# Scattered rows added on VectorE behind the gate products of the last expert pairs, the results of the last two groups summed in PSUM, tokens scaled during the output projection

## The chip, the core and the metric

The kernel runs on one core of one Trainium2 chip. The metric is the device time of one execution in microseconds, here called us; lower is better. Five engines work side by side and meet at semaphores: TensorE (PE, with its weight loads as PEld), VectorE (DVE), ScalarE (ACT), GpSimd (POOL) and SyncE (SP). SP issues nearly all loads of weights; POOL issues the gathers and scatters of rows whose place is known only at run time.

## The reference

Two layers work on 256 latent and 256 context tokens, each 1024 wide. A layer first mixes tokens (attention and a long convolution, left out here) and then runs a mixture of 32 experts, two for each token:

```python
x = x + g1 * _merge(attn, hyena, gates, w_br_a, w_br_b, w_out)      # output projection
h2 = _rms(x, norm_ffn) * (1.0 + sc2) + sh2                          # scaled tokens
x = x + g2 * _hier_moe(h2, w_group, b_group, w_router, b_router, moe_w1, moe_w3, moe_w2)
...
# for every expert e, with cw = the routing weight of the token for e
hid = silu(h2 @ w1[e]) * (h2 @ w3[e]) * cw
y = y + hid @ w2[e]
```

All is float32. Layer 0 does this for the latent and the context tokens, layer 1 for the latent tokens alone.

## The kernel before

**Tiles.** Tokens stand in tiles of 128 rows: four in layer 0 (tiles 0 and 1 latent, 2 and 3 context), two in layer 1. The output projection runs in two halves of 512 columns; for each half and tile, PE leaves a product in PSUM, DVE multiplies it by the gate `g1` and adds it to `x`, PE transposes `x`, multiplies it by the router's weights, and ACT squares it for the norm.

**Routing.** `moe` then forms `rs` (one over the root mean square) and the logits `lg`, runs a chain of small operations on DVE (all called `rtr` in the trace), and sends the scaled tokens `h2` to DRAM: `x*rs*sc2` by DVE, except for the last tile, which ACT and POOL do, and for every tile the addition of `sh2` by POOL. The chain ends in `gi`, the row numbers with which POOL gathers `xg`, the rows of one quad of experts, back from DRAM.

**Experts.** `first_round` walks over 8 quads q of 4 experts, that is 16 pairs of experts, counted here as p = 0 to 15 (quad q has the pairs 2q and 2q+1). For each pair, `w13` multiplies the gathered rows by two weights (PE, L1414, into `pW`), ACT takes `sl`, DVE forms the gate product `hd` (L1369, in `hidden`), PE transposes it into `pX` (L1372), ACT copies it to `hdT`, and `w2` multiplies by the third weight (PE, L1429). For q < 6 ACT copies the result `Y` to SBUF and POOL scatters its rows to `ybuf` in DRAM. After that, `collect` gathers them for each token tile (two DMAs of 512 KB: `yr` for even tiles of layer 0, `yt` for the rest), POOL adds the two (L220 on POOL), and DVE multiplies by `g2` (`bc`) and adds to `x`. For q = 6 and 7 nothing is scattered: `combine` multiplies `Y` by a matrix `PT` of zeros and ones on PE (L1462, into the PSUM banks G and Q), each quad for itself, and `residual` multiplies that by `g2` and adds it to `x` (`xg` and `x` of 512 columns on DVE).

**Order.** The code is given to a scheduler that fixes each engine's order beforehand; every engine then takes its instructions strictly in that order. A weight of 1 MB (96 in a layer) is loaded by `fetch` into the next slot of a ring as soon as the slot's last reader has been issued. The ring has 14 slots in layer 0 and 16 in layer 1. `yt` and the tokens `h2` share a pool of two buffers (`T4`).

## Time and profile before

| | |
|---|---|
| Time, median of 3 runs | 1466.85 us (1466.72 to 1468.5) |
| Profiled execution | 1467.82 us, of which span 1466.0 us |
| PE, DVE, ACT, POOL busy | 88%, 46%, 31%, 17% of the span |
| Mean granted PE clock | 0.954 of full speed |
| Experts of layer 0 | about 611 to 907 us of the span |
| Experts of layer 1 | about 1211 to 1457 us |

The busy shares are means over stages with different limits. In the middle of both expert stages the DMA engines are saturated and PE is hardly ever idle; at their ends this is not so, and there one has to look at which wait ends last. Times below are positions in the span, in us.

### The profile page before, as it was taken

The page shows a single profiled execution, that of the slowest core. Times are in us where ns is not written, and L with a number is a line of the kernel's source. Part 1 is how long each engine was busy: PE and PEld are TensorE (multiplying, and loading weights), DVE is VectorE, ACT ScalarE, POOL GpSimd, SP SyncE. Part 2 cuts the span into 40 slices and gives each one's busy share as a digit, 9 for nine tenths or more (in the row PEclk, how much of TensorE's full clock was granted, in tenths as well). Part 3 has the DMA queues.
Part 4 walks back from the last instruction along what each step waited for, and adds up shares of the span by engine and source line. Part 5 has one row for each costly group of instructions (what it writes and reads, how often), then busy time and mean ns, then how long its engine had stood idle before and what let it go on. Part 6 is the DMA issues. An engine that isn't in the chain of part 4 may idle for free. (4 is left out here: it accounts for less than half of the span.)

```text
span 1466.0 us, 18236 instructions
## 1 busy us (share of the span) xinstructions
PE 1294.2 (88%) x7071; PEld 831.8 (57%) x7071; DVE 672.0 (46%) x1365; ACT 450.8 (31%) x882; POOL 255.2 (17%) x193
## 2 busy tenths in 40 slices
PE   5999999999999999499988487899899949998886
PEld 2555778876577987244322123899779933433232
DVE  4654366666677655601000235774774771000014
ACT  3433222336622232122111002543575412221110
POOL 2021042360000003311101301122600031111010
PEclk8999999999999999599999788999999979999999
DMA  9645534554278663699999943343426757999992
GB/s 377 270 167 193 209 113 161 186 224 173 86 253 306 230 258 141 218 403 420 419 420 423 418 166 122 128 144 145 173 73 232 252 181 292 421 418 419 421 417 106
DMA packets 65691, 373.04 MB, mean 254 GB/s; under 512 B 11994, under 2 KB 13338, under 8 KB 26048
## 3 DMA queue, kind: packets, MB, share of 16 engines
q1 hardware_dynamic: 54368, 347.67, 60.9%
q0 software_dynamic: 10368, 21.02, 3.9%
q10 hardware_dynamic: 864, 3.15, 0.5%
q8 instruction: 57, 0.93, 0.2%
q14 instruction: 34, 0.28, 0.1%
HBM read 362.06 MB, written 27.53 MB: 266 GB/s over the span
## 5 line engine op out<-in xcount | busy, mean ns | idle before, releaser
L1414 PE MATMUL pW<-we,xT 128*64 128x512 f32 x1024 | 265.7, 609 | 13.1 <-DMA we<-in_wexp_dram 12.9
L1414 PEld LDWEIGHTS pW<-we,xT 128*64 128x64 f32 x1024 | 80.1, 139 | 158.0 <-issue 135.6
L1369 DVE SCALAR_TENSOR_TENSOR hd<-sl,cws,pW 128x256 f32<-128x256 f32 x32 | 15.3, 479 | 326.0 <-ACT sl L223 326.0
L239 PE MATMUL pA<-hT,wsp 128*128 128x512 f32 (+1 forms) x448 | 156.7, 350 | 3.9 <-ACT hf L223 3.9
L241 PE MATMUL pA<-hT,wsp 128*128 128x512 f32 (+1 forms) x448 | 154.8, 345 | 1.1 <-DVE wsp L220 1.1
L240 PE MATMUL pA<-hT,wsp 128*128 128x512 f32 (+1 forms) x448 | 154.5, 345 | 0.0
L220 DVE TENSOR_TENSOR wsp<-win,wsp 128x1024 fp32r<-128x1024 f32 x80 | 100.9, 1269 | 107.8 <-ACT wsp L223 107.6
L1429 PE MATMUL pW<-we,hdT 128*64 128x512 f32 x512 | 141.3, 616 | 4.9 <-ACT hdT L223 4.7
L223 ACT ACTIVATE wsp<-win 128x1024 fp32r<-128x1024 f32 x80 | 84.0, 1057 | 139.8 <-PE pA L241 136.2
L240 PE MATMUL pA<-wsp,hT 128*128 128x256 f32 x352 | 100.4, 285 | 2.5 <-DVE wsp L220 2.5
L239 PE MATMUL pA<-wsp,hT 128*128 128x256 f32 x352 | 100.8, 286 | 0.7 <-ACT vv L223 0.7
L241 PE MATMUL pA<-wsp,hT 128*128 128x256 f32 x352 | 100.4, 285 | 0.0
L239 PEld LDWEIGHTS pA<-hT,wsp 128*128 128x128 f32 x448 | 86.3, 193 | 21.7 <-issue 8.0
L240 PEld LDWEIGHTS pA<-hT,wsp 128*128 128x128 f32 x448 | 86.3, 193 | 13.8 <-issue 6.1
L241 PEld LDWEIGHTS pA<-hT,wsp 128*128 128x128 f32 x448 | 86.2, 192 | 11.3 <-issue 1.8
L1429 PEld LDWEIGHTS pW<-we,hdT 128*64 128x64 f32 x512 | 47.7, 141 | 74.1 <-issue 60.0
L223 ACT ACTIVATE sl<-pW 128x256 f32<-128x256 f32 x32 | 12.3, 384 | 238.0 <-PE pW L1414 238.0
L223 ACT ACTIVATE Y<-pW 128x512 f32<-128x512 f32 (+1 forms) x64 | 38.2, 598 | 141.0 <-PE pW L1429 125.0
L239 PEld LDWEIGHTS pA<-wsp,hT 128*128 128x128 f32 x352 | 68.1, 194 | 5.3 <-issue 2.5
L240 PEld LDWEIGHTS pA<-wsp,hT 128*128 128x128 f32 x352 | 68.1, 193 | 3.4 <-DVE wsp L220 3.1
L248 POOL TENSOR_TENSOR rs<-rsq,mh 128x1 f32<-128x1 f32 x14 | 11.6, 830 | 332.8 <-DVE rsq L247 331.8
L241 PEld LDWEIGHTS pA<-wsp,hT 128*128 128x128 f32 x352 | 68.2, 194 | 0.2
(301 smaller groups left out, 2377.6 us busy)
## 6 DMA issues: line engine op xcount, KB each, us to landing
we<-in_wexp_dram SPq DMA_DIRECT2D x190, 1024.0 KB
win<-in_win_dram SPq DMA_DIRECT2D x40, 1024.0 KB
ada<-in_ada_dram SPq DMA_DIRECT2D x32, 1024.0 KB
ada<-in_adaj_dram SPq DMA_DIRECT2D x16, 1024.0 KB
wbr<-in_wbr_dram SPq DMA_DIRECT2D x8, 1024.0 KB
wout<-in_wout_dram SPq DMA_DIRECT2D x8, 1024.0 KB
ybuf<-zero SPq DMA_DIRECT2D x12, 512.0 KB
bc<-modd SPq DMA_DIRECT2D x12, 512.0 KB
```

The lines of the kernel that those rows point to most:

```text
L220: (eng or self.nc.vector).tensor_tensor(out=out, in0=a, in1=b, op=op)
L223: self.nc.scalar.activation(out, in_, func, **kw)
L239: self.nc.tensor.matmul(out, lh, rh, start=start, stop=False)
L240: self.nc.tensor.matmul(out, lh, rl, start=False, stop=False)
L241: self.nc.tensor.matmul(out, ll, rh, start=False, stop=stop)
L248: nc.gpsimd.tensor_tensor(out=out, in0=t, in1=self.mh[:, : shape[1]], op=ALU.pow)
L1369: nc.vector.scalar_tensor_tensor(out=hd, in0=sl, scalar=cws, in1=pa[:, 256:512], op0=ALU.mult, op1=ALU.mult)
L1414: nc.tensor.matmul(pa[64 * e : 64 * e + 64, :], xT[:, kc, cs], wt[(2 * p + e, kc // 4)][:, kc % 4, :], start=kc == 0, stop=kc == KC - 1)
L1429: nc.tensor.matmul(py[64 * e : 64 * e + 64, :], hdT[:, fc, 64 * e : 64 * e + 64], wt[(2 * p + e, 2)][:, fc, hs], start=fc == 0, stop=fc == 1)
```

## The change

The change has six parts. (1) The tokens `h2` are formed in the loop of the output projection, on DVE alone; the loads of `sc2` and `sh2` come there too. (2) The two first `xg` buffers are zeroed by ACT (a copy with scale 0) instead of a POOL memset. (3) `collect` handles one tile at a time and returns the additions as a function; the two gathered halves are added on DVE. The gathers of the first half of the tiles are issued as before, after the second weight of pair 12; their additions are written behind `hidden` of pair 14. The gathers of the other tiles are written there too, and their additions behind `hidden` of pair 15. `g2` is loaded later. (4) The ring of layer 0 has slot 0 as a fifteenth for its first four rounds. (5) For tiles 0 and 1 the products of quads 6 and 7 are summed in one PSUM bank each, which is held from quad 6 to the end; for tiles 2 and 3 all eight products are done at the end. There is one `residual` for each tile and half in place of two. (6) Slots of some split weights change.

```diff
@@ output projection
+        h2 = [sc2b[:, i // 2, :] if i % 2 else self.T4([P, D], name="h2") for i in range(nt)]
...
                 self.tt(x_, x_, xg, ALU.add)
+                self.tt(h2[i][:, hs], x_, sc2b[:, i // 2, hs], ALU.mult)
...
+                if half:
+                    self.tt(ssq[i][:, 0:1], ssq[i][:, 0:1], ssq[i][:, 1:2], ALU.add)
+                    self.rsq(rss[i], ssq[i][:, 0:1], D, [P, 1])
+                    V.scalar_tensor_tensor(out=h2[i], in0=h2[i], scalar=rss[i], in1=sh2b[:, i // 2, :],
+                                           op0=ALU.mult, op1=ALU.add)
+                    nc.scalar.dma_start(self.rows[l][i * P : i * P + P, :], h2[i])
+                    V.scalar_tensor_tensor(out=lg[:, i, :], in0=lg[:, i, :], scalar=rss[i], in1=bb[:, i // 2, :],
+                                           op0=ALU.mult, op1=ALU.add)
@@ moe
-            if i < nt - 1:
-                V.scalar_tensor_tensor(out=h2, in0=x_, scalar=rss[i], in1=sc_, op0=ALU.mult, op1=ALU.mult)
-            else:
-                self.act(h2, x_, scale=rss[i])
-                self.tt(h2, h2, sc_, ALU.mult, nc.gpsimd)
-            self.tt(h2, h2, sh2b[:, i // 2, :], ALU.add, nc.gpsimd)
-            nc.scalar.dma_start(hd2[i * P : i * P + P, :], h2)
@@ pull
-                nc.gpsimd.memset(xg, 0.0)
+                self.act(xg, self.ones[:, 0:1].unsqueeze(2).to_broadcast([P, 2, D]), scale=0.0)
@@ collect
-                self.tt(ya, ya, yt[1], ALU.add, nc.gpsimd)
-                self.tt(ya, ya, g2[:, i // 2, :], ALU.mult)
-                self.tt(x_, x_, ya, ALU.add)
+            def add():
+                x_ = xm[i // 2][:, i % 2, :]
+                self.tt(yt[0], yt[0], yt[1], ALU.add)
+                self.tt(yt[0], yt[0], g2[:, i // 2, :], ALU.mult)
+                self.tt(x_, x_, yt[0], ALU.add)
+            return add
@@ first_round
             ring = [10, 11, 12, 13, 19, 20, 4, 5, 6, 7, 8, 9, 16, 18]
+            seq = (ring + [0]) * 4 + ring * 3
...
+        def add(q, i, half):
+            hs = slice(half * 512, half * 512 + 512)
+            for j in range(2):
+                for x in range(2):
+                    nc.tensor.matmul(held[i, half], quads[q]["PT"][j][:, i, :], quads[q]["Y"][j][:, x, hs],
+                                     start=q == 6 and j + x == 0, stop=q == 7 and j + x == 2)
...
             hdT = self.hidden(w13(2 * q, z["xT"], fill), z["cw"][:, 0:1])
+            if q == 7:
+                for u in adds:
+                    u()
+                adds = [collect(i) for i in range(nt // 2, nt)]
...
             if q == 6:
-                collect()
+                adds = [collect(i) for i in range(nt // 2)]
...
             hdT = self.hidden(w13(2 * q + 1, z["xT"], fill), z["cw"][:, 1:2])
+            if q == 7:
+                for u in adds:
+                    u()
...
-        for u in fill + last[6:] + combine(7):
+        for u in fill:
             u()
+        for i, half in units:
+            add(7, i, half)
+            residual(i, half, held[i, half], 7)
+        for i in range(2, nt):
+            for half in range(2):
+                held[i, half] = self.ps("G" if i == 2 else "Q")
+                for q in (6, 7):
+                    add(q, i, half)
+                residual(i, half, held[i, half], 7)
```

The diff does not tell where the scheduler puts these instructions. On DVE, in layer 0, from the gate product of pair 11 to that of pair 13 or just before it, the order was this (`x_4404` holds tiles 0 and 1, `x_4407` tiles 2 and 3):

```order
L1369 SCALAR_TENSOR_TENSOR hd_6037<-sl_6035,cws_5462,pW_5991 128x256
L220 TENSOR_TENSOR yr_6131<-yr_6131,bc_5008 128x1024
L220 TENSOR_TENSOR x_4404<-x_4404,yr_6131 128x1024
L1369 SCALAR_TENSOR_TENSOR hd_6123<-sl_6121,cws_5629,pW_6077 128x256
L220 TENSOR_TENSOR yt_6137<-yt_6137,bc_5008 128x1024
L220 TENSOR_TENSOR x_4404<-x_4404,yt_6137 128x1024
L220 TENSOR_TENSOR Y_6130<-pW_6159,Y_6130 128x512
L220 TENSOR_TENSOR Y_6130<-pW_6168,Y_6130 128x512
L220 TENSOR_TENSOR yr_6131<-yr_6131,bc_5008 128x1024
L220 TENSOR_TENSOR x_4407<-x_4407,yr_6131 128x1024
L220 TENSOR_TENSOR yt_6149<-yt_6149,bc_5008 128x1024
L220 TENSOR_TENSOR x_4407<-x_4407,yt_6149 128x1024
```

In the changed kernel, the same place from the gate product of pair 11 to that of pair 14 reads:

```order
L1365 SCALAR_TENSOR_TENSOR hd_6036<-sl_6034,cws_5463,pW_5990 128x256
L220 TENSOR_TENSOR yr_6133<-yr_6133 128x1024
L220 TENSOR_TENSOR yt_6136<-yt_6136,yt_6137 128x1024
L1365 SCALAR_TENSOR_TENSOR hd_6122<-sl_6120,cws_5630,pW_6076 128x256
L220 TENSOR_TENSOR Y_6129<-pW_6143,Y_6129 128x512
L220 TENSOR_TENSOR Y_6129<-pW_6152,Y_6129 128x512
L1365 SCALAR_TENSOR_TENSOR hd_6185<-sl_6183,cws_5630,pW_6140 128x256
L220 TENSOR_TENSOR Y_6192<-pW_6229,Y_6192 128x512
L220 TENSOR_TENSOR Y_6192<-pW_6238,Y_6192 128x512
L1365 SCALAR_TENSOR_TENSOR hd_6259<-sl_6257,cws_5797,pW_6226 128x256
```

Although the additions are written behind the gate product of pair 14, the first one of each of the tiles 0 and 1 stands ahead of the gate product of pair 12. That of pair 13, which had all of tiles 2 and 3 ahead of it, has nothing of them ahead of it any more.

From there to the gate product of pair 15, the changed kernel's DVE has the rest of tiles 0 and 1, and all of tiles 2 and 3:

```order
L220 TENSOR_TENSOR yr_6133<-yr_6133,bc_6130 128x1024
L220 TENSOR_TENSOR yt_6136<-yt_6136,bc_6130 128x1024
L220 TENSOR_TENSOR x_4404<-x_4404,yr_6133 128x1024
L220 TENSOR_TENSOR x_4404<-x_4404,yt_6136 128x1024
L220 TENSOR_TENSOR Y_6279<-pW_6283,Y_6279 128x512
L220 TENSOR_TENSOR Y_6279<-pW_6292,Y_6279 128x512
L220 TENSOR_TENSOR yr_6272<-yr_6272 128x1024
L220 TENSOR_TENSOR yr_6272<-yr_6272,bc_6130 128x1024
L220 TENSOR_TENSOR yt_6275<-yt_6275,yt_6276 128x1024
L220 TENSOR_TENSOR x_4407<-x_4407,yr_6272 128x1024
L220 TENSOR_TENSOR yt_6275<-yt_6275,bc_6130 128x1024
L220 TENSOR_TENSOR x_4407<-x_4407,yt_6275 128x1024
```

Behind these stands the gate product of pair 15. Six operations of tiles 2 and 3, which were done ahead of pair 13 on POOL and DVE, have moved between pairs 14 and 15. POOL issues the gathers of tiles 2 and 3 in the order `yt_6275`, `yr_6272` twice, `yt_6276`, and the first waits for DVE to release the buffers of tiles 0 and 1.

In layer 1 DVE had, from the gate product of pair 11 to the first addition of gathered rows:

```order
L1369 SCALAR_TENSOR_TENSOR hd_10714<-sl_10712,cws_10155,pW_10668 128x256
L1369 SCALAR_TENSOR_TENSOR hd_10800<-sl_10798,cws_10314,pW_10754 128x256
L220 TENSOR_TENSOR Y_10807<-pW_10827,Y_10807 128x512
L220 TENSOR_TENSOR Y_10807<-pW_10836,Y_10807 128x512
L1369 SCALAR_TENSOR_TENSOR hd_10871<-sl_10869,cws_10314,pW_10824 128x256
L220 TENSOR_TENSOR Y_10878<-pW_10915,Y_10878 128x512
L220 TENSOR_TENSOR Y_10878<-pW_10924,Y_10878 128x512
L1369 SCALAR_TENSOR_TENSOR hd_10945<-sl_10943,cws_10473,pW_10912 128x256
L220 TENSOR_TENSOR yt_10810<-yt_10810,bc_10808 128x1024
```

In the changed kernel it is this:

```order
L1365 SCALAR_TENSOR_TENSOR hd_10685<-sl_10683,cws_10126,pW_10639 128x256
L220 TENSOR_TENSOR yt_10781<-yt_10781,yt_10782 128x1024
L1365 SCALAR_TENSOR_TENSOR hd_10771<-sl_10769,cws_10285,pW_10725 128x256
L220 TENSOR_TENSOR Y_10778<-pW_10788,Y_10778 128x512
L220 TENSOR_TENSOR Y_10778<-pW_10797,Y_10778 128x512
L1365 SCALAR_TENSOR_TENSOR hd_10832<-sl_10830,cws_10285,pW_10785 128x256
L220 TENSOR_TENSOR Y_10839<-pW_10876,Y_10839 128x512
L220 TENSOR_TENSOR Y_10839<-pW_10885,Y_10839 128x512
L1365 SCALAR_TENSOR_TENSOR hd_10906<-sl_10904,cws_10444,pW_10873 128x256
```

Here, too, the first addition, that of tile 0 (`yt_10781`), now stands ahead of the gate product of pair 12 (`hd_10771`), where DVE had nothing that waited for a gather.

## Rows read from the trace of the kernel before

**Rows 1.** Windows of 40 us: busy us (instructions) by engine, clock, DMA share, GB/s.

```profile
800.00:840.00 40.00, 17.45 (x64) 5.39 (x60) 8.94 (x9) 2.35 (x5) 11.41 (x11) 0.79 1.02 418
840.00:880.00 40.00, 30.23 (x95) 10.78 (x96) 14.20 (x20) 3.54 (x7) 2.34 (x1) 0.87 0.45 183
1400.00:1440.00 40.00, 34.35 (x129) 11.88 (x130) 6.92 (x10) 2.73 (x6) 5.42 (x4) 0.96 0.91 372
```

**Rows 2.** Timeline of PE, layer 0's last pairs: start, us, engine, operation [idle before].

```profile
820.52 0.69 PE L1372 MATMUL pX<-cst,hd 128*128 128x128 f32 x2 [18.16 <-DVE hd L1369]
846.15 0.69 PE L1372 MATMUL pX<-cst,hd 128*128 128x128 f32 x2 [8.71 <-DVE hd L1369]
```

**Rows 3.** Timeline of POOL, the same place.

```profile
803.06 1.18 POOL L1313 DMA_DIRECT2D yr<-ybuf  x2 [7.05 <-DMA ybuf<-Y,gi]
822.74 2.35 POOL L220 TENSOR_TENSOR yt<-yt,yt 128x1024 f32<-128x1024 f32 x1 [4.31 <-DMA yt<-ybuf]
840.84 2.34 POOL L220 TENSOR_TENSOR yt<-yt,yt 128x1024 f32<-128x1024 f32 x1 [5.18 <-DMA yt<-ybuf]
```

**Rows 4.** Timelines of DVE and ACT, the same place (gate products of pairs 12 to 15).

```profile
819.99 0.47 DVE L1369 SCALAR_TENSOR_TENSOR hd<-sl,cws,pW 128x256 f32<-128x256 f32 x1
825.12 1.23 DVE L220 TENSOR_TENSOR yt<-yt,bc 128x1024 f32<-128x1024 f32 x1 [4.66 <-POOL yt L220]
837.48 0.39 ACT L223 ACTIVATE sl<-pW 128x256 f32<-128x256 f32 x1 [10.35 <-PE pW L1414]
845.62 0.47 DVE L1369 SCALAR_TENSOR_TENSOR hd<-sl,cws,pW 128x256 f32<-128x256 f32 x1
869.53 0.48 DVE L1369 SCALAR_TENSOR_TENSOR hd<-sl,cws,pW 128x256 f32<-128x256 f32 x1 [2.58 <-ACT sl L223]
890.30 0.48 DVE L1369 SCALAR_TENSOR_TENSOR hd<-sl,cws,pW 128x256 f32<-128x256 f32 x1 [8.38 <-ACT sl L223]
```

**Rows 5.** Groups on PE from 870 to 890: busy us, mean ns | idle before.

```profile
L1414 PE MATMUL pW<-we,xT 128*64 128x512 f32 x32 | 8.4, 600 | 0.0
L1429 PE MATMUL pW<-we,hdT 128*64 128x512 f32 x16 | 5.6, 605 | 0.5 <-ACT hdT L223 0.5
L1462 PE MATMUL pG<-Y,PT 128*128 128x512 f32 x14 | 4.9, 432 | 0.3 <-DVE xg L220 0.3
L1462 PE MATMUL pQ<-Y,PT 128*128 128x512 f32 x2 | 0.8, 422 | 0.0
```

**Rows 6.** The same from 846 to 869.5.

```profile
L1462 PE MATMUL pG<-Y,PT 128*128 128x512 f32 x16 | 5.6, 439 | 1.7 <-DVE xg L220 1.6
```

**Rows 7.** Timeline of POOL, layer 1's last pairs.

```profile
1394.41 1.17 POOL L1313 DMA_DIRECT2D yt<-ybuf  x2 [7.66 <-DMA ybuf<-Y,gi]
1406.68 2.35 POOL L220 TENSOR_TENSOR yt<-yt,yt 128x1024 f32<-128x1024 f32 x1 [11.09 <-DMA yt<-ybuf]
```

**Rows 8.** Timelines of DVE and PE, the same place (gate products of pairs 12 to 15).

```profile
1393.24 0.48 DVE L1369 SCALAR_TENSOR_TENSOR hd<-sl,cws,pW 128x256 f32<-128x256 f32 x1 [13.42 <-ACT sl L223]
1403.41 8.78 PE L1414 MATMUL pW<-we,xT 128*64 128x512 f32 x30 [3.37 <-DMA we<-in_wexp_dram]
1412.64 0.48 DVE L1369 SCALAR_TENSOR_TENSOR hd<-sl,cws,pW 128x256 f32<-128x256 f32 x1 [12.32 <-ACT sl L223]
1426.64 0.48 DVE L1369 SCALAR_TENSOR_TENSOR hd<-sl,cws,pW 128x256 f32<-128x256 f32 x1 [7.22 <-ACT sl L223]
1447.81 0.47 DVE L1369 SCALAR_TENSOR_TENSOR hd<-sl,cws,pW 128x256 f32<-128x256 f32 x1
```

**Rows 9.** Routing, timelines of POOL and DVE in both layers.

```profile
586.83 4.76 POOL L220 TENSOR_TENSOR h<-h,bc 128x1024 f32<-128x1024 f32 x2 [1.26 <-ACT h L223]
589.45 2.37 DVE L220 TENSOR_TENSOR rtr<-rtr 128x16 f32<-128x16 f32 x3
592.07 0.17 DVE L220 TENSOR_TENSOR rtr<-rtr 128x16 f32<-128x16 f32 x1
1191.81 2.40 DVE L220 TENSOR_TENSOR rtr<-rtr 128x8 f32<-128x8 f32 x3
1194.44 2.00 DVE L220 TENSOR_TENSOR rtr<-rtr 128x8 f32<-128x8 f32 x1
1196.47 1.83 DVE L1121 TENSOR_SCALAR rtr<-rtr 128x8 f32<-128x8 f32 x1
```

More of the change, by code (lines that the diff above doesn't have):

```diff
@@ L899, in layer @@
             xm = self.xres
+        if full:
+            sc2b = self.bcast(l, 2, 17, ns)
+            sh2b = self.bcast(l, 1, 18, ns)
+        else:
+            b2 = self.S(10, [P, 2, D], name="bc")
+            for s in range(2):
+                nc.sync.dma_start(b2[:, s, :], self.modd[l, 2 - s, 0:1, :].partition_broadcast(P)[:, 0, :])
+            sc2b, sh2b = b2[:, 0:1, :], b2[:, 1:2, :]
+        h2 = [sc2b[:, i // 2, :] if i % 2 else self.T4([P, D], name="h2") for i in range(nt)]
         ssq = [self.st([P, 2], "ss", 4) for i in range(nt)]
+        rss = [self.st([P, 1], "rs", 4) for i in range(nt)]
         for half in range(2):
@@ L1390, in first_round @@
             order[84:] = [(e, k) for e in range(28, 32) for k in range(2)] + [(e, 2) for e in range(28, 32)]
-            ring = [15, 18, 11, 13, 16, 21, 2, 3, 17, 19, 4, 5, 6, 7, 8, 9]
-        nr = len(ring)
+            seq = [15, 18, 11, 13, 16, 21, 2, 3, 17, 19, 4, 5, 6, 7, 8, 9] * 6
+        prev = [max([-1] + [m for m in range(n) if seq[m] == seq[n]]) for n in range(96)]
         def fetch():
-            while ri[0] < 96 and (ri[0] < nr or order[ri[0] - nr] in done):
-                (e, k), s = order[ri[0]], ring[ri[0] % nr]
+            while ri[0] < 96 and (prev[ri[0]] < 0 or order[prev[ri[0]]] in done):
+                (e, k), s = order[ri[0]], seq[ri[0]]
                 ri[0] += 1
@@ L1487, in first_round @@
             if q == 6:
-                collect()
+                adds = [collect(i) for i in range(nt // 2)]
             if q == 7:
-                last = combine(6)
-                fill += last[:6]
+                fill += [lambda x=x: open_(*x) for x in units]
             hdT = self.hidden(w13(2 * q + 1, z["xT"], fill), z["cw"][:, 1:2])
+            if q == 7:
+                for u in adds:
+                    u()
             if q > 5:
```

77 lines of the change are left out of this document (26 added, 51 removed).

## The prediction

> **What bounds the kernel now.** The page gives PE 88% of the span, so I looked for the places where PE is not busy, stage by stage, in windows of 40 us. In the middle of an expert stage there is nothing to win: the DMA engines are saturated with weights and PE keeps up. The ends differ. In the window from 800 to 840 PE is busy for 17.45 of 40 us, while in layer 1's window from 1400 to 1440 it is busy for 34.35 [rows 1]. So the loss stands at the end of layer 0, and PE's timeline there says on what: 18.16 us ahead of pair 12's transposes and 8.71 us ahead of pair 13's, both put down to the gate product `hd` on DVE [rows 2]. DVE is no busy engine there; it waits in turn. Ahead of the gate products of pairs 12 and 13 stand multiplications of gathered rows, which wait for POOL's additions, and those wait for gathers that crawl beside the weights: the four issued from 803 on have all landed only at 822.74, about 19.7 us later, and tile 3's at 840.84 [rows 3]. ACT's `sl` of pair 13 ended at 837.9, its gate product started at 845.62 [rows 4]: 7.7 us lost to the gathers of tiles 2 and 3 alone. In layer 1 the same gathers cost nothing at pair 12: its gate product, at 1393.24, waited for `sl` [rows 8], although the rows landed at 1406.68 [rows 7], since POOL alone stood waiting.
>
> **Routing.** Beside POOL's two additions at 586.83, three `rtr` operations of DVE took 2.37 us, where one undisturbed takes 0.17; in layer 1 five of them took 2.40 + 2.00 + 1.83 us [rows 9]. The change takes these additions from POOL. In layer 0 three operations at about 0.2 save 1.8 us. The other new work (two operations of 512 columns and one of 1024 for each tile, together about 2.5 us at the 1.23 of [rows 4] for 1024) fills DVE's waits for PE in the loop. Only the last tile's operation of 1024 now stands ahead of `lg`. In layer 0 the operations beside it were themselves slowed by POOL, which I let pay for it: 0. In layer 1, five operations at 0.2 save 5.2, and the last tile's operation with a short one ahead of it costs 1.4: 3.8 saved. I keep 0.5 to 4.5 us for each layer as bounds. The zeroing moves to ACT, which like POOL waits for PE there; it is hidden behind the chain of `rtr` operations, and would cost its length, some 2 us for each layer, if ACT had to do it within that chain. The fifteenth slot brings one load (1 MB, 2.5 us at the 418 GB/s of [rows 1]) earlier; PE was not waiting for weights at that place, so it is 0, at best −2.5.
>
> **Layer 0's end.** I follow the four gate products on the clock of before.
> Pair 12 now has the additions of tiles 0 and 1 ahead of it, the second of which needs the rows that landed at 822.74. With 1.8 us from the routing and 1.23 for the addition [rows 4], it starts at 822.2, 2.2 *later* than before. The big stall stays.
> Pair 13: from 819.99 to the end of `sl` at 837.9 PE took 17.9 us; less 0.4, because nothing delays DVE's `Y`, it comes at 839.7 instead of 845.62: −5.9.
> Pair 14: I build it from the interval between pairs 14 and 15, which was 20.8 us [rows 4]. In it 16 matmuls with `PT` took 5.7 us, 0.35 each, and 0.3 us of waiting [rows 5]. Without them a pair takes 14.8. From pair 13 to 14 I count about 10 of them in the new order (3.5 us) and 1.4 for waiting for `Y`: 19.7, so 859.4 instead of 869.53: −10.1. The interval was 23.9 because, besides 16 matmuls with `PT`, PE waited 1.7 us for `xg` [rows 6], which goes with quad 6's own residual, and began after a wait of 8.71 [rows 2].
> Pair 15: 8 such matmuls, 14.8 + 2.8 = 17.6: PE is ready at 877.0 instead of 890.30: −13.3.
> Now the price: six operations for tiles 2 and 3 stand ahead of pair 15. DVE is through with tiles 0 and 1 at 859.4 + 0.5 + 4 × 1.23 = 864.8, and only then POOL may issue the gathers (four, 2.1 MB). Weights no longer fill the queues: from 840 to 880 the mean was 183 GB/s [rows 1]. No row shows four gathers alone. At 418 GB/s they take 5.0 us; beside the weights 19.7. The first condition is nearer, so I take 7: landed at 871.8, and the last four operations (4.9) end at 876.7, just as PE is ready. After pair 15 the DVE work is the same (four products with `xg`, four sums, four `rest`), and PE's larger remainder hides behind it: 0. Layer 0 ends 13.3 us earlier.
>
> The Trainium skill, DMA: Bandwidth & Descriptors, section on the anatomy of one DMA from GpSimd, puts such a DMA at about 2 us plus its bytes at 436 GB/s. By that, as an estimate, four overlapping gathers land 6.8 us after issue, and layer 1's two after 4.4, which would make the sum 1 us better. The trace does not bear it out beside weights: two gathers took 12.3 us [rows 7]. No run here shows it for gathers alone.
>
> **Layer 1's end.** Here the change *adds* a wait. The addition of tile 0 stands ahead of pair 12's gate product, and PE, which is in order, has the transposes, the second weight and all of pair 13 queued behind it. With 3.8 us from the routing the rows land at 1402.9; plus 1.23 gives 1404.1 for pair 12 instead of 1393.24: +10.9. Part is given back, since pair 13 had to wait 3.37 us for weights and ran slowly (8.78) [rows 8]: with the 14.0 us of the next pair and 0.7 for two more `PT` matmuls it comes at 1418.8 instead of 1412.64, +6.2. Pair 14: 14.0 + 1.4, 1434.2, +7.6. From pair 14 to 15 PE took 18.0 us; about 5 fewer `PT` matmuls and no wait for `xg` make 15.8: 1450.0. The gathers of tile 1 are issued when DVE releases the buffers, at 1434.7 + 2 × 1.23 = 1437.2. Two beside weights took 12.3; weights end there (372 GB/s mean in the last window), at 418 GB/s it would be 2.5; I take 9, nearer the row that has two of them. Then three operations (3.7) and `Y` (1.3): pair 15 at 1451.2 instead of 1447.81, +3.4. The rest, 18.2 us to the end of the span, is unchanged.
>
> **Sum.** −13.3 + 3.4 = −9.9 against the profiled execution of 1467.8: 1457.9. The median of the runs is 1.0 below it, so 1457.
>
> **The rivals.**
> *More than that.* The gathers land after 5.0 and 2.5 us, so only PE counts: layer 1's pair 15 at 1450.0 (+2.2). If a pair in layer 0 also takes the 14.0 of layer 1 rather than 14.8 for the bare work, twice 0.8, both routings give their best (2.7 and 0.7 more) and the slot 2.5: −9.9 − 1.2 − 1.6 − 3.4 − 2.5 = −18.6, 1448. With the second weight's 5.6 us shrunk by another 2 in each of two pairs, as the stretches without other matmuls inside may allow, 1444. For it: the emptied queues. Against: nothing had asked so much of DVE between pairs 14 and 15.
> *Gathers crawl to the end: slower.* If SP's next loads fill the queues as weights did, layer 0's four gathers need 19.7 us: landed at 884.5, pair 15 at 889.4, −0.9. Layer 1's two need 12.3: 1449.5, pair 15 at 1454.5, +6.7. Together +5.8: 1473. It decides from about 12 us for layer 0's gathers and 12 for layer 1's on, where the sum is 0. For it: every gather shown so far was that slow. Against: the queue's 183 GB/s.
> *Nothing comes of it.* The weights' stream sets both ends, and the stalls at 820 and 846 only covered waiting for weights; the routing's gain disappears in the ring, and layer 1's wait is absorbed too: 1465 to 1469. Against: from 840 to 880 the queues moved 183 GB/s in the mean [rows 1], less than half of what they can, so layer 0's weights end well ahead of pair 15 at 890.30.
>
> **Numbers.** Forecast 0.52 (1451 to 1462), more 0.25, nothing 0.10, slower 0.13. A measurement here tells about 0.2%, 2.9 us, from no change. So faster 0.77, same 0.10, slower 0.13. The range, leaving out the crawl's end and a little below, is 1444 to 1468.
>
> **What would show it.** In the profile after: `rtr` operations of 0.2 us and no additions on POOL; pair 12's transposes in layer 0 still ending a wait of 18 to 20 us, pair 13's no more than 1; the gathers of tiles 2 and 3 landing about 7 us after issue, with pair 15's gate product released by `sl` and not by them, at about 13 us ahead of before; in layer 1 a new wait of some 13 us of PE ahead of pair 12, of which 3 to 4 us are left at pair 15. I am wrong if PE waits long ahead of pair 15, if layer 1's wait is paid in full (+8), or if the gathers at 803 land at another pace than before, since both new waits hang on it.

## The result, and the profile after

The changed kernel takes 1443.51 us (median of 4 runs, 1441.07 to 1444.38) where the kernel before takes 1467.67 (1466.72 to 1469.4): a ratio of 0.9831, 95% interval 0.9814 to 0.9848. That is 24.2 us faster, 9.9 were forecast, and the time lies 0.5 us below the range. The profiled execution took 1441.07 us, span 1439.3.

First the windows that answer to [rows 1], with one of layer 1 added in which its new wait lies (columns as there):

```profile
800.00:840.00 40.00, 24.97 (x83) 8.59 (x83) 6.09 (x8) 3.54 (x7) 0.54 (x1) 0.77 0.95 389
840.00:880.00 40.00, 34.65 (x135) 14.00 (x133) 19.53 (x22) 6.88 (x12) 1.57 (x3) 0.96 0.45 176
1360.00:1400.00 40.00, 24.62 (x91) 9.39 (x88) 4.53 (x7) 3.92 (x8) 1.70 (x3) 0.79 1.01 417
1400.00:1440.00 40.00, 28.48 (x121) 11.39 (x119) 14.84 (x20) 3.92 (x8) 0.54 (x1) 0.91 0.24 90
```

Layer 0's end is still a place where PE is busy 25 of 40 us, and layer 1 has got one like it. PE's timeline at the transposes of pairs 12 to 15 of layer 0 and of pair 12 of layer 1, which answers to [rows 2], says on what it waits:

```profile
812.97 0.69 PE L1368 MATMUL pX<-cst,hd 128*128 128x128 f32 x2 [22.84 <-DVE hd L1365]
831.03 0.44 PE L1368 MATMUL pX<-cst,hd 128*128 128x128 f32 x2 [0.99 <-DVE hd L1365]
849.37 0.44 PE L1368 MATMUL pX<-cst,hd 128*128 128x128 f32 x2 [0.99 <-DVE hd L1365]
867.95 0.44 PE L1368 MATMUL pX<-cst,hd 128*128 128x128 f32 x2 [3.39 <-DVE hd L1365]
...
1376.11 0.69 PE L1368 MATMUL pX<-cst,hd 128*128 128x128 f32 x2 [13.81 <-DVE hd L1365]
```

And DVE's timeline, with one row of ACT, which answers to [rows 4] and [rows 8], says what DVE waits for there (the gate products themselves follow at once):

```profile
811.30 1.23 DVE L220 TENSOR_TENSOR yt<-yt,yt 128x1024 f32<-128x1024 f32 x1 [6.29 <-DMA yt<-ybuf]
812.44 0.48 DVE L1365 SCALAR_TENSOR_TENSOR hd<-sl,cws,pW 128x256 f32<-128x256 f32 x1
...
860.36 1.22 DVE L220 TENSOR_TENSOR yr<-yr 128x1024 f32<-128x1024 f32 x1 [5.02 <-DMA yr<-ybuf]
...
864.60 0.38 ACT L223 ACTIVATE sl<-pW 128x256 f32<-128x256 f32 x1 [9.98 <-PE pW L1411]
867.42 0.47 DVE L1365 SCALAR_TENSOR_TENSOR hd<-sl,cws,pW 128x256 f32<-128x256 f32 x1
...
1374.43 1.23 DVE L220 TENSOR_TENSOR yt<-yt,yt 128x1024 f32<-128x1024 f32 x1 [26.72 <-DMA yt<-ybuf]
1375.57 0.48 DVE L1365 SCALAR_TENSOR_TENSOR hd<-sl,cws,pW 128x256 f32<-128x256 f32 x1
...
1415.91 1.23 DVE L220 TENSOR_TENSOR yt<-yt,yt 128x1024 f32<-128x1024 f32 x1 [4.08 <-DMA yt<-ybuf]
```

Nearly all this the prediction had. Two things it had not. Pair 15's gate product of layer 0 was not released by `sl`, which ended at 864.98: the additions of tiles 2 and 3 held it until 867.42, 2.4 us longer. And the long waits cost more than their length: the transposes behind them take 0.69 us where the others take 0.44, since the granted clock was still 0.50, in layer 0 until 818.2:

```profile
812.90:818.20 5.30, 4.75 (x12) 1.69 (x14) 0.02 (x1) 0.38 (x1) 0.46 (x1) 0.50 0.95 391
```

To see where the rest comes from, I take the starts of the same instructions in both profiles, and for each stretch between two of them how much shorter or longer it became (us):

| stretch | forecast | measured |
|---|---|---|
| up to the output projection of layer 0 (not touched by the change) | 0 | −2.7 |
| from there to `gi`, layer 0 | −1.8 | −2.8 |
| `gi` to pair 0 | 0 | **−4.5** |
| pair 0 to 11 | 0 | **−1.6** |
| 11 to 12, 12 to 13 | +4.0, −8.1 | +4.1, −7.6 |
| 13 to 14, 14 to 15 | −4.2, −3.2 | −5.6, −2.2 |
| pair 15 to the head of layer 1 (`xn`) | 0 | **−3.7** |
| head of layer 1 to its `gi` | −3.8 | −3.9 |
| `gi` to pair 11, layer 1 | 0 | −1.7 |
| 11 to 12, 12 to 13 | +14.7, −4.7 | +14.4, −2.0 |
| 13 to 14, 14 to 15 | +1.4, −4.2 | +2.0, **−8.4** |
| pair 15 to the end | 0 | −0.6 |

The sum is −26.8 between the profiles. The first row belongs to no part of the change: in the profiles below, all with the same code up to there, it ends anywhere from 541.5 to 545.7.

The routing came as forecast: `rtr` operations that took 2.4 us beside POOL's additions [rows 9] are short again, in DVE's timeline of either layer:

```profile
585.91 0.38 DVE L220 TENSOR_TENSOR rtr<-rtr 128x16 f32<-128x16 f32 x3
...
1166.27 0.37 DVE L220 TENSOR_TENSOR rtr<-rtr 128x8 f32<-128x8 f32 x3
```

Two of the bold rows can be read in the profiles at once. Behind the routing stood these before, in the timeline of PE (its first product of pair 0) and of SP's queue, and in windows of 5 us:

```profile
608.30 0.88 PE L1282 MATMUL pG<-cst,xg 128*128 128x128 f32 x3 [3.17 <-DMA xg<-h2d,gi]
577.81 0.80 SPq L394 DMA_DIRECT2D bc<-modd  x2
581.77 1.29 SPq L212 DMA_DIRECT2D we<-in_wexp_dram  x3
597.79 0.34 SPq L1251 DMA_DIRECT2D posd<-prm  x1
598.23 0.38 SPq L1252 DMA_DIRECT2D cwd<-rtr  x1
598.66 0.90 SPq L212 DMA_DIRECT2D we<-in_wexp_dram  x2
```

```profile
595.00:600.00 5.00, 1.05 (x26) 0.85 (x25) 4.95 (x19) 0.20 (x1) 0.00 (x0) 0.50 0.26 61
600.00:605.00 5.00, 1.09 (x32) 1.01 (x32) 4.43 (x15) 0.00 (x0) 3.29 (x3) 0.50 0.90 359
```

SP issues nothing for 14.7 us, because its next entries are the stores `posd` and `cwd`, which wait for the routing. The queues run empty (61 GB/s), and then two loads of 1 MB start 2.4 and 1.9 us ahead of the gather issued at 601.10, which takes 7.2 us (counted here and below from its issue to PE's first product). After the change the same two timelines have this:

```profile
600.44 0.90 PE L1273 MATMUL pG<-cst,xg 128*128 128x128 f32 x3 [0.85 <-DMA xg<-h2d,gi]
573.20 12.67 SPq L212 DMA_DIRECT2D we<-in_wexp_dram  x6
592.26 0.34 SPq L1242 DMA_DIRECT2D posd<-prm  x1
592.70 0.38 SPq L1243 DMA_DIRECT2D cwd<-rtr  x1
593.13 0.42 SPq L212 DMA_DIRECT2D we<-in_wexp_dram  x1
```

Six loads are out before the stores, `g2` (`bc`) has gone from the place, and one load is left behind them: the gather, issued at 596.13, takes 4.3 us.

At the end of layer 0, POOL's `rs` for the first tiles of the next layer stood beside three subtractions for split weights on DVE before:

```profile
909.05 3.91 POOL L248 TENSOR_TENSOR rs<-rsq,mh 128x1 f32<-128x1 f32 x1 [1.96 <-DVE rsq L247]
909.05 3.49 DVE L220 TENSOR_TENSOR wsp<-win,wsp 128x1024 fp32r<-128x1024 f32 x3
913.04 1.42 DVE L457 TENSOR_SCALAR xn<-x,rs 128x1024 f32<-128x1024 f32 x2 [0.50 <-POOLq L1354]
```

Afterwards it stands alone, and the subtractions come behind `xn`:

```profile
884.99 0.55 POOL L248 TENSOR_TENSOR rs<-rsq,mh 128x1 f32<-128x1 f32 x1 [1.65 <-DVE rsq L247]
886.45 1.42 DVE L457 TENSOR_SCALAR xn<-x,rs 128x1024 f32<-128x1024 f32 x2 [0.58 <-DVEq L1350]
887.78 1.22 DVE L220 TENSOR_TENSOR wsp<-win,wsp 128x1024 fp32r<-128x1024 f32 x1
```

### The profile page after: what moved, and what is told of

It is laid out like the page before. It is cut to its first block, busy times and chain, and to the rows that moved or that the text cites. A ratio compares the mean times of both kernels' runs of the same rounds, so it can differ in the third digit from the quotient of the medians.

```text
span 1439.3 us, 18183 instructions
## 1 busy us (share of the span) xinstructions
PE 1281.0 (89%) x7071; PEld 831.1 (58%) x7071; DVE 660.3 (46%) x1361; ACT 455.8 (32%) x884; POOL 211.0 (15%) x175
## 5 line engine op out<-in xcount | busy, mean ns | idle before, releaser
L1365 DVE SCALAR_TENSOR_TENSOR hd<-sl,cws,pW 128x256 f32<-128x256 f32 x32 | 15.3, 480 | 305.9 <-ACT sl L223 305.9
L239 PEld LDWEIGHTS pA<-hT,wsp 128*128 128x128 f32 x448 | 86.2, 192 | 21.6 <-issue 8.0
L223 ACT ACTIVATE sl<-pW 128x256 f32<-128x256 f32 x32 | 12.3, 383 | 218.7 <-PE pW L1411 218.7
L248 POOL TENSOR_TENSOR rs<-rsq,mh 128x1 f32<-128x1 f32 x14 | 8.4, 601 | 424.9 <-DVE rsq L247 414.0
```

Source lines behind the costliest of these rows:

```text
L223: self.nc.scalar.activation(out, in_, func, **kw)
L239: self.nc.tensor.matmul(out, lh, rh, start=start, stop=False)
L248: nc.gpsimd.tensor_tensor(out=out, in0=t, in1=self.mh[:, : shape[1]], op=ALU.pow)
L1365: nc.vector.scalar_tensor_tensor(out=hd, in0=sl, scalar=cws, in1=pa[:, 256:512], op0=ALU.mult, op1=ALU.mult)
```

## The experiments

Every kernel was timed beside the kernel before on the same chip (its median there was 1466.0 to 1467.4). "Changed" is the kernel after. Differences from it are between medians of different timings; taken by the ratios they come out up to 2.1 us otherwise. "The head of layer 1" is PE's first product with `xn`.

**Where the additions stand.** If pair 12 waits only because the first additions are ahead of its gate product, holding them behind that of pair 14 must give back both waits. `issue_after` makes the scheduler place what stands in it behind the instruction named.

```diff
 # late14
-                for u in adds:
-                    u()
+                with self.tc.issue_after(self.hd.ins):
+                    for u in adds:
+                        u()
                 adds = [collect(i) for i in range(nt // 2, nt)]
```

> The changed kernel, with the first additions of tiles 0 and 1 (tile 0 in layer 1) kept behind the gate product of pair 14, where the code writes them; nothing else moves. If the wait ahead of pair 12 (22.84 us of PE in layer 0, 13.81 in layer 1) is a loss of the end, as the prediction held, it disappears and pair 12 starts about 20 and 12 us earlier; since weights still arrive until about 843 and 1409 and the gathers of the later tiles still stand ahead of pair 15, I expect about 8 us less in layer 0 and 5 in layer 1: 1430, within 5. If the weights set the ends anyway, the wait only moves to the weights and to pair 15: 1443, within 2.

Measured: 1427.76 us, ratio 0.9733 (0.9717 to 0.9750). Pair 12 comes 16.1 us behind pair 11 in layer 0 (37.3 in the changed kernel) and 13.9 in layer 1 (28.3). The granted clock is 1.00 there, from 800 to 818. Part of it returns at pair 15 of layer 0, 26.9 behind pair 14 instead of 18.6: DVE stands ahead of its gate product for the gathers of tiles 2 and 3.

```profile
848.00 1.22 DVE L220 TENSOR_TENSOR yr<-yr 128x1024 f32<-128x1024 f32 x1 [10.21 <-DMA yr<-ybuf]
```

late15 also puts these last additions behind the gate product of pair 15:

```diff
 # late15, as well
             if q == 7:
-                for u in adds:
-                    u()
+                with self.tc.issue_after(self.hd.ins):
+                    for u in adds:
+                        u()
```

> As late14, and the additions of tiles 2 and 3 (tile 1 in layer 1) are kept behind the gate product of pair 15. In the changed kernel pair 15 started 2.8 us after ACT's product of layer 0 was there, and DVE is idle for 6 us behind it. If the gathers of the later tiles bound pair 15, this brings 3 to 8 us over late14: about 1424. If they are not late at pair 15, it is equal to late14 within 2.

Measured: 1421.62, ratio 0.9694 (0.9679 to 0.9709). Pairs 14 and 15 are 16.7 apart, but the head of layer 1 now comes 26.5 us behind pair 15 instead of 19.8: DVE makes the additions there, is busy for 21.0 of these 26.5 us and waits 3.7 for the gathers. The profiles of late14 and late15 differ by 1.5 us only, as late14's is of its fastest run; where the rest of the 6.1 us between the medians lies is not shown.

late13 goes the other way: first additions behind pair 13, the last ones behind pair 14, and `g2` loaded two pairs sooner, so that the late gathers leave sooner.

```diff
 # late13
+            if q == 5:
+                collect(-1)          # loads g2
@@ behind the second hidden of the loop
+            if q == 6:
+                with self.tc.issue_after(self.hd.ins):
+                    for u in adds:
+                        u()
+                adds = [collect(i) for i in range(nt // 2, nt)]
```

> The changed kernel with the additions of the first half of the tiles held behind the gate product of pair 13, those of the second half behind that of pair 14, and `g2` loaded behind pair 11, so that the gathers of the second half leave some 15 us sooner. Theory (the wait for gathers is a matter of where the additions stand): no wait for gathered rows ahead of pair 12, pair 15 of layer 0 about 846 where late14 had 856, pair 15 of layer 1 about 3.8 us closer to pair 14: 1414, 12 to 14 below late14. Rival: gathers sent sooner share the queues with weights and delay the pairs as much: 1421 to 1428, like the two kernels before it.

Measured: 1424.57, ratio 0.9712 (0.9693 to 0.9732). The forecast of 1414 missed, the rival was right: the gathers do leave sooner, at 819 to 824, but PE waits for weights even before that, with `g2` (loaded from 776 on) and the first gathers in the queues, the late gathers take up to 16.6 us, and `Y` still comes late behind the additions.

```profile
804.50 5.35 PE L1412 MATMUL pW<-we,xT 128*64 128x512 f32 x16 [2.64 <-DMA we<-in_wexp_dram]
812.03 3.65 PE L1412 MATMUL pW<-we,xT 128*64 128x512 f32 x14 [2.17 <-DMA we<-in_wexp_dram]
846.78 0.80 PE L1457 MATMUL pG<-Y,PT 128*128 128x512 f32 x1 [3.87 <-DVE Y L220]
```

**Which engine adds.** One argument puts the addition of the two gathered halves back on POOL, all else as in the changed kernel:

```diff
 # after_pooladd
-                self.tt(yt[0], yt[0], yt[1], ALU.add)
+                self.tt(yt[0], yt[0], yt[1], ALU.add, nc.gpsimd)
```

> The changed kernel with the title's first part alone undone: the two gathered halves are added by POOL again. The scheduler then has nothing that waits for gathers ahead of the gate products of pairs 12 to 14. Theory (what costs at pair 12 is that DVE, in order, waits for the gathers; POOL may wait at no cost): pair 12 of layer 0 comes 16 us behind pair 11 instead of 37, that of layer 1 14 to 16 instead of 28; part is paid at pair 15 of layer 0, whose additions wait as in late14: 1426 to 1430. Rival: the wait for gathers only moves to the multiplications by `g2`, and POOL's additions slow DVE besides: 1443 or more.

Measured: 1427.54, ratio 0.9731 (0.9707 to 0.9755). The title's first item alone *costs* 16.0 us by the medians, 14.7 by the ratios. PE's timeline has the four pairs of layer 0, then two of layer 1:

```profile
792.61 0.44 PE L1368 MATMUL pX<-cst,hd 128*128 128x128 f32 x2 [0.99 <-DVE hd L1365]
812.93 0.44 PE L1368 MATMUL pX<-cst,hd 128*128 128x128 f32 x2 [0.99 <-DVE hd L1365]
831.26 0.44 PE L1368 MATMUL pX<-cst,hd 128*128 128x128 f32 x2 [0.99 <-DVE hd L1365]
856.90 0.69 PE L1368 MATMUL pX<-cst,hd 128*128 128x128 f32 x2 [9.37 <-DVE hd L1365]
1355.22 0.44 PE L1368 MATMUL pX<-cst,hd 128*128 128x128 f32 x2 [0.99 <-DVE hd L1365]
1374.58 0.44 PE L1368 MATMUL pX<-cst,hd 128*128 128x128 f32 x2 [0.99 <-DVE hd L1365]
```

POOL meanwhile waits for the very same gathers, and nobody waits for these two additions:

```profile
804.72 2.33 POOL L220 TENSOR_TENSOR yr<-yr 128x1024 f32<-128x1024 f32 x1 [9.79 <-DMA yr<-ybuf]
812.24 2.35 POOL L220 TENSOR_TENSOR yt<-yt,yt 128x1024 f32<-128x1024 f32 x1 [5.19 <-DMA yt<-ybuf]
```

late15_pool is late15 with the same edit, but POOL's addition stands in `collect`, not in `add`, so that it is not held back:

```diff
+            self.tt(yt[0], yt[0], yt[1], ALU.add, nc.gpsimd)
             def add():
                 x_ = xm[i // 2][:, i % 2, :]
-                self.tt(yt[0], yt[0], yt[1], ALU.add)
```

> late15 with the two gathered halves added by POOL, as in the kernel before; only the multiplications by `g2` and the additions to `x` are held behind the gate products of pairs 14 and 15. Theory: behind pair 15 of layer 0 DVE is what bounds, and it loses 2.5 us of work; two of the four late gathers also leave sooner: 1418, 2 to 4 below late15. Rival: POOL's additions stand between the landing and DVE (2.35 us each) and eat that: 1421 to 1424.

Measured: 1418.03, ratio 0.9671 (0.9650 to 0.9691), 3.6 below late15 (their intervals overlap) and the best kernel here, 25.5 us below the changed one. The head of layer 1 follows pair 15 by 21.3 us instead of 26.5.

**The parts alone.** In these the hunks of the named parts, as the diff of the change has them, are put into the kernel before, and nothing else. The code that loads `g2` in `collect` belongs to part 3 as well as to part 4. Parts 1 and 2 (tokens, zeroing) only:

> The kernel before with parts 1 and 2 of the change alone (tokens scaled in the loop of the output projection, zeroing on ACT); ring, additions and sums of the layers' ends as before. The prediction's terms give -1.8 and -3.8, 1462. The theory from the two traces (the front of an expert stage gains beyond the routing chain, since no load waits any more for a slot that POOL's additions hold, so that fewer bytes stand ahead of the gather of pair 0) gives about -3 and -4 for the routing and -3 to -4 more between `gi` and pair 0 of layer 0: about 1456. If the front's gain is due to the fifteenth slot instead, it is not seen here and the time is 1460 or more.

before_tokens: 1460.31, ratio 0.9942 (0.9929 to 0.9955), where the rival had put it and 4 us above the theory. `gi` of both layers comes 2.9 and 4.1 us sooner after the projection, as the theory had it. The gather of pair 0 takes 6.5 us instead of 7.2, so the shorter gather is only partly the work of these two.

Parts 3 and 5 (additions, sums) only:

> The kernel before with parts 3 and 5 alone (additions on DVE by tile, sums in PSUM); routing and ring as before. The scheduler then places the additions of tiles 2 and 3 ahead of pair 14 instead of pair 15. The prediction's terms less its routing give about -11.5 for layer 0 and about +5 to +7 for layer 1: 1459 to 1462. If the gain behind pair 15 of layer 0 (3.7 us in the changed kernel) belongs to these parts too, 2 to 4 less: 1456 to 1459. If the parts need the emptier queue that the rest of the change leaves, the time is 1464 or more.

before_ends: 1457.80, ratio 0.9924 (0.9911 to 0.9937). Pairs 11 to 15 take 91.1 us in layer 0 (103.6 before) and 74.9 in layer 1 (68.5).

Part 5 (sums) only:

> The kernel before with part 5 alone: sums of quads 6 and 7 in PSUM, no residual of quad 6, additions of gathered rows on POOL and ahead of pairs 12 and 13 as before. The prediction's steps give nothing up to pair 13, about -4 at pair 14 (1.7 us of waiting for `xg`, six products fewer) and -7 at pair 15 of layer 0, -2 to -5 in layer 1: 1455 to 1458. Rival: PE only waits elsewhere for weights, 1462 or more.

before_psum: 1452.10, ratio 0.9898 (0.9878 to 0.9917), 3 us better than expected. Pairs 11 to 15 take 95.8 us in layer 0 and 64.7 in layer 1, and the way from pair 15 to the head of layer 1 is 2.2 us shorter: 13.8 in all. The rest of the 15.3 lies in stretches that it does not touch. Its pair 12 still waits in layer 0 as in [rows 2].

Part 3 (additions by tile on DVE) only:

> The kernel before with part 3 alone: additions by tile on DVE. The scheduler puts tile 0's three operations and the first of tile 1 ahead of pair 12 of layer 0, tiles 2 and 3 ahead of pair 14, and in layer 1 the first addition ahead of pair 12. By the prediction's steps +4 at pair 12 and -3 to -6 from pair 13 on in layer 0, then +11 at pair 12 of layer 1, of which 3 to 6 stay at pair 15: 1464 to 1469, no clear gain. Rival: additions away from POOL are a gain by themselves: 1458 to 1461.

before_collect: 1467.73, ratio 1.0011 (0.9999 to 1.0024), no gain: pairs 11 to 15 of layer 0 take 5.4 us less, those of layer 1 8.8 more.

Parts 4 and 6 (fifteenth slot, `g2` loaded late, other slots for split weights) only, POOL adding as before:

> The kernel before with parts 4 and 6 alone: slot 0 as the fifteenth of layer 0's ring (with `g2` loaded in `collect`), and the other slots of the split weights. The prediction's terms say 0, 1467. The theory from the traces gives -2.2 between pairs 4 and 5 of layer 0, where with fourteen slots an interval of 16.9 stands and with fifteen one of 14.7 to 15.9, and -3.4 between pair 15 of layer 0 and the output projection of layer 1: 1461 to 1462. If the fifteenth slot pays only together with tokens that come sooner, 1464.

before_ring: 1443.97, ratio 0.9844 (0.9824 to 0.9863): as much as the whole change, where both theories had 6 at most. Pairs 4 and 5 are 14.7 us apart (16.9 before), and the head of layer 1 follows pair 15 by 18.8 us (23.6); but 18.1 us come from the pairs 11 to 15 of layer 0 (the profile, of its fastest run, is 29.9 us shorter in all). Slot 0 now holds weights for four rounds, and `g2` can be loaded only when the last of them has been read. In before_collect the code loads `g2` at the same place, but no weight stands in slot 0, and SP loads it before the experts begin. SP's queue in before_ring, then in before_collect:

```profile
814.57 4.08 SPq L394 DMA_DIRECT2D bc<-modd  x2
...
596.16 0.90 SPq L394 DMA_DIRECT2D bc<-modd  x2
```

With the late load the scheduler puts all that multiplies by `g2` behind the gate product of pair 14. Nothing of DVE's that waits for gathers is ahead of pairs 12 and 13 any more. In before_collect, with the early load, multiplications still stand ahead of both.

Whether that order or the slot does it, before_late14 tells: ring, slots and POOL's additions of the kernel before, with `g2` loaded in `collect` (SP issues it at 596.6, as slot 0 holds no weights), and

```diff
 # before_late14: multiplications by g2 and additions to x, by half of the tiles
+            if q == 7:
+                with self.tc.issue_after(self.hd.ins):
+                    for u in adds:
+                        u()
```

behind `hidden` of pairs 14 and 15.

> The kernel before, ring of fourteen and additions on POOL as there, with one thing moved: the multiplications by `g2` and the additions to `x` of the first half of the tiles stand behind the gate product of pair 14, those of the second half behind that of pair 15 (`g2` is loaded in `collect`). Theory: the large gain of parts 4 and 6 alone comes from the order on DVE, which follows from the later load of `g2`, and not from the fifteenth slot: pairs 12 and 13 16 and 19 us apart here too, 1440 to 1446. Rival: the gain belongs to the slot and the freed loads: 1455 or more.

Measured: 1448.76, ratio 0.9884 (0.9861 to 0.9907). It lies 3 us above the range that the theory gave and well below its rival. Pairs 11 to 15 of layer 0 take 86.2 us (85.5 in before_ring), with pair 12 at 16.1: the order does it. Pair 15 is late in both, 33.2 us behind pair 14 here and 31.3 in before_ring, since DVE comes to the residual of quad 6, whose bank PE waits for, only after the late additions: in before_ring it stands behind DVE's own, here the trace puts its wait of 12.3 us down to POOL's addition of `yt`. PE in before_late14:

```profile
861.34 1.22 PE L1468 MATMUL pG<-Y,PT 128*128 128x512 f32 x2 [9.18 <-DVE xg L220]
```

That residual is what part 5 takes away.

**What is behind the unpriced stretches.** before_posd is the kernel before with the two stores issued by ACT:

```diff
-        nc.sync.dma_start(posd, pos[:, 0:nt, :])
-        nc.sync.dma_start(cwd, cw)
+        nc.scalar.dma_start(posd, pos[:, 0:nt, :])
+        nc.scalar.dma_start(cwd, cw)
```

> The kernel before with the two small stores of positions and weights (`posd`, `cwd`) issued by ACT instead of SP, so that no load of weights stands behind them on SP. Theory: two of the loads come as late as 0.2 us ahead of the gather of pair 0 and take its bandwidth; earlier, they are through by then, and pair 0 comes 2 to 3 us sooner: 1464 to 1465. Rival: those loads wait for slots that POOL's additions hold, not for the stores, and the queue stays as full: 1467, no change. Against both, a store that ACT must wait for could hold `sl` of pair 0: slower.

Measured: 1464.83, ratio 0.9983 (0.9970 to 0.9996): 2.5 us (0.6 to 4.4 by the interval), small but as expected. SP's timeline and the windows show the mechanism:

```profile
581.56 11.43 SPq L212 DMA_DIRECT2D we<-in_wexp_dram  x5
```

```profile
595.00:600.00 5.00, 1.04 (x26) 0.85 (x25) 4.98 (x20) 0.20 (x1) 0.00 (x0) 0.50 0.98 407
600.00:605.00 5.00, 1.23 (x32) 1.06 (x32) 4.25 (x15) 0.00 (x0) 3.52 (x3) 0.50 0.35 106
```

The two loads are issued at 585.8 and 592.7 and are nearly through when the gather leaves, at 600.87; it takes 5.0 us. In the kernel before they went out 2.4 and 1.9 us ahead of it, not 0.2.

sh2_pool is the changed kernel with the addition of `sh2` back on POOL:

```diff
-                    V.scalar_tensor_tensor(out=h2[i], in0=h2[i], scalar=rss[i], in1=sh2b[:, i // 2, :],
-                                           op0=ALU.mult, op1=ALU.add)
+                    V.tensor_scalar(out=h2[i], in0=h2[i], scalar1=rss[i], scalar2=None, op0=ALU.mult)
+                    self.tt(h2[i], h2[i], sh2b[:, i // 2, :], ALU.add, nc.gpsimd)
```

> The changed kernel with one thing put back: the addition of `sh2` is done by POOL again (still in the loop of the output projection), and DVE only multiplies by `rs`. Theory: what costs is POOL's addition beside DVE's chain of small operations and the slot that it holds, so most of the front's gain goes: 3 us for each layer, 1449. Rival: the gain comes from having the work done in the loop, whichever engine adds: 1443 to 1445.

Measured: 1449.32, ratio 0.9873 (0.9859 to 0.9888), as the theory had it. DVE's small operations beside POOL's addition at 587.37 (2.34 us) are slow again, three that take 0.38 us in the changed kernel:

```profile
587.70 2.25 DVE L220 TENSOR_TENSOR rtr<-rtr 128x16 f32<-128x16 f32 x3
```

and the gather of pair 0 takes 6.5 us.

ring14 is the changed kernel with fourteen slots. `g2` is loaded at the same place of the code, but it is not late any more, other than the expectation says: slot 0 holds no weights, and SP loads it at 595.6, 3 us ahead of the gather of pair 0.

```diff
-            seq = (ring + [0]) * 4 + ring * 3
+            seq = ring * 7
```

> The changed kernel with the old ring of 14 slots in layer 0; slot 0 holds only g2, still loaded late. If the fifteenth slot is why the first gathered rows of layer 0 landed 4.3 us after their gather's issue instead of 7.2 (a load less in the queues ahead of them) and why the middle of layer 0 gained 1.6, this loses 3 to 5 us: 1447. If the slot does nothing, as I predicted (0, at best -2.5), it is 1443.5 within 2.

Measured: 1447.04, ratio 0.9869 (0.9852 to 0.9886), 3.5 above the changed kernel (5.6 by the ratios). Pairs 4 and 5 are 16.9 us apart instead of 14.7; the kernels with the slot have 14.7 to 15.9, those without 16.9 to 17.3. The gather takes 5.0 us instead of 4.3, but late15_pool, with the slot, has 5.0 too. On DVE all of tiles 0 to 3 is done ahead of pair 13 again. So the run undoes the slot, the late `g2` and the order that follows, and does not price the slot alone.

win1211 is the changed kernel with the early split weights in slots 12 and 11 as before.

```diff
-            wsp = self.S((8, 9)[n], [P, 2, KC, P], F32R, name="wsp")
+            wsp = self.S((12, 11)[n], [P, 2, KC, P], F32R, name="wsp")
```

> The changed kernel with the early split weights of layer 1 in slots 12 and 11, as before, instead of 8 and 9. The change gained 3.7 us between pair 15 of layer 0 and the first matmul of layer 1, where I had predicted 0; in the kernel before, POOL's rs of tile 1 took 3.91 us beside three subtractions of DVE for split weights, in the changed one 0.55. If the slots decide where the scheduler puts those subtractions, this loses about 3: 1446.5. If the gain is from quad 6's residual, it is 1443.5 within 1.5.

Measured: 1450.39, ratio 0.9888 (0.9867 to 0.9908), 6.9 above it. A subtraction again stands ahead of `xn`, and the head of layer 1 comes 21.3 us behind pair 15 instead of 19.8. This shows 1.5 of the 6.9. Pieces of 1.8 to 1.9 lie in the pairs 0 to 11 of either layer and in the start of layer 1, on code that is the same: other profiles show both levels there too. For layer 1 the end of the next section shows what differs; where the others come from stays open.

## Why the prediction was wrong

**The ends of the layers.** The waits at pairs 12 to 14 came as the prediction put them, in kind and mostly in size. The first gathers, on which they hang, landed 19.8 us after issue in layer 0 and 12.2 in layer 1 (19.7 and 12.3 before). At pair 15 of layer 0 the additions, and not `sl`, came last, by 2.4 us. Pairs 11 to 15 of layer 0 were to become 11.5 us shorter and became 11.3; those of layer 1 were to become 7.2 longer and became 6.0; within them single intervals missed by up to 4.2 us and made up for each other. Layer 0's late gathers landed about 7 us after issue, as chosen: the first is issued at 853.0, and DVE adds at 860.36. But only three left then, one of the four having found its buffer free at 812.8. The Trainium skill, DMA: Bandwidth & Descriptors, section on the anatomy of one DMA from GpSimd, gives 5.6 us for three, as an estimate; the trace has 1.7 more, beside loads of `win`. The queues were not empty, as the mean of 183 GB/s had made it seem: from 853 to 860.3 they moved 413 GB/s. That 7 us held is luck, three gathers for four in fuller queues. In layer 1, too, one of the two had left early, at 1375.95, and the other, issued at 1412.12, landed 3.8 us later, where 9 had been taken. The term of +3.4 for pair 15 was mis-sized by that, and because PE alone took 12.8 us from pair 14 to 15 and not 15.8: eight products with `PT` stood in that stretch before and none after, where the prediction took off five.

**The step that failed** is that outside the layers' ends only the routing got a price; three terms were put at nothing, and 9.8 of the 16.9 us that the profiles gained beyond the forecast lie there (−4.5, −1.6 and −3.7 in the table). First the slot. "The fifteenth slot brings one load (1 MB, 2.5 us at the 418 GB/s of [rows 1]) earlier; PE was not waiting for weights at that place, so it is 0, at best −2.5": pairs 4 to 5 become 2.2 us shorter with it, pairs 0 to 11 of layer 0 1.6 (over all profiles 158.7 to 161.9 us with the slot, 161.5 to 163.9 without). Its larger effect is that it makes `g2` late: the order that follows is worth 17.6 us by itself (before_late14), but little in the changed kernel, where additions on DVE wait ahead of pair 12 anyhow (pairs 11 to 15 take 92.3 us, 92.8 in ring14).

"After pair 15 [...] 0": 3.7 us. Part 5 alone, in which DVE has one residual of the last quads to make and not two, gives 2.2; parts 4 and 6 alone give 4.8; with the old slots 1.5 of the 3.7 go. These shares do not add up, but both parts act there, part 6 by where subtractions stand against `xn`, and part 6 had no term at all.

And nothing was said of the gather of pair 0, 4.5 us with the clock: I looked at what the routing chain computes, not at what SP's queue does meanwhile. Of these 4.5, 2.3 are the gather (from `gi` to PE's first product 7.75, now 5.42); the gathers of before, before_tokens, ring14 and the changed kernel took 7.2, 6.5, 5.0 and 4.3 us. The slot with the late `g2` alone gives nothing (7.6 in before_ring), nor does `g2` behind the stores (7.2 in before_ends); the tokens alone give 0.7, and the rest comes only with the parts together. Which load in SP's queue decides it is shown for the two stores (before_posd), not for each part. The other 2.1 are the clock, discussed below.

Of the 16.9 us, 2.7 lie ahead of all that the change touches. They, the 2.1 of the clock and the 1.7 of layer 1 (below) cannot be put down to the change. They are more than the 0.5 us by which the time lies below the range: that it fell outside is in part chance.

**What the tracing of each step did not show** is that the change holds a large gain and gives most of it back. The sums alone gain 15.3 us, parts 4 and 6 alone 23.5, the tokens 7.0; the additions on DVE alone nothing. All of them together give 24.2, and all but the engine of the additions 38.8. The wait that the prediction saw in both layers ("The big stall stays", "the change *adds* a wait") is the price of that engine, without a return: in after_pooladd POOL waits for the same gathers at no cost, and in before_ring the late `g2`, which needs slot 0 in the ring, clears pair 12 with POOL's additions as they were. In layer 0 it is a price only beside the late `g2`: with the early one (before_collect) pairs 11 to 15 take 5.4 us less there, since multiplications hold pair 12 anyhow; in layer 1 they take 8.8 more. The prediction compared the order of before with that of after, and so never asked which single edit had put each instruction where it stood.

**The rivals.** "More than that" came nearest: 1444 to 1451, by gathers that land fast, the slot and both routings. It was near in part by luck: the gathers did land fast in layer 1, but not in layer 0, and the routings gave 1.0 and 0.1 us more than forecast, not 2.7 and 0.7. "Gathers crawl to the end" is refuted for the changed kernel by 7 and 3.8 us, but late13 and late14 show its mechanism: issued while weights still flow, the same gathers took up to 16.6 us (late13) and kept DVE waiting 10.2 (late14). Its threshold was mis-added: with 12 us for the gathers of both layers the prediction's steps give −8.6 + 6.4 = −2.2, and the sum is 0 only from about 14 us in layer 0. "Nothing comes of it" is refuted. The 1.7 us of layer 1 between `gi` and pair 11 belong to no part: pairs 0 to 11 of layer 1 take 155.6 to 158.1 us in all these profiles, with the same code. What differs is where PE must wait for a weight. Pairs 10 to 11 take 17.8 us in ring14 (first row) and 14.0 in the changed kernel:

```profile
1346.71 8.75 PE L1411 MATMUL pW<-we,xT 128*64 128x512 f32 x30 [2.63 <-DMA we<-in_wexp_dram]
1339.70 7.08 PE L1411 MATMUL pW<-we,xT 128*64 128x512 f32 x30 [0.49 <-DMA we<-in_wexp_dram]
```

In ring14 the granted clock was 0.50 for 3.4 us from 1346.7 on; in the changed kernel such a place stands at 1306.4, between pairs 8 and 9 (19.7 us, 16.9 in ring14). Why the weight comes late now here, now there, is not shown.

## What to carry to other kernels

An instruction that waits for a transfer belongs on an engine behind which nobody queues: moving a cheap addition from an idle engine to one in the critical chain cost about 15 us, though the addition itself was faster there (1.23 us against 2.35). Read also what each queue holds back behind an entry that waits: moving two small stores to another queue was worth 2.5 us. And when a scheduler orders the work, vary single edits: here one more slot in a ring made the load of one operand late, and the order that followed moved more time than any arithmetic.
